# A two-layer mixer trunk in split fp32: order of work between VectorE and ScalarE, two budgets in the planner, smaller weight loads

## The chip, the cores and the metric

One Trainium2 chip, one of its cores. The metric is device time in microseconds of one execution of the program: the median of three executions of the kernel before is 2058.87 us (2057.31 to 2063.75).

## What is computed

Two layers, each on 256 tokens of 2048 channels, all in float32: one RMS norm, one input projection to nine parts, a convolution branch and an attention branch, each gated and projected, and an output projection with the residual.

```python
def conv_branch(a, glu, gate, conv_w, conv_b, ln_g, ln_b):
    u = a * jax.nn.sigmoid(glu)
    u = causal_depthwise_conv(u, conv_w) + conv_b          # 31 taps, 2048 channels
    u = jax.nn.silu(layernorm(u, ln_g, ln_b))
    return u * jax.nn.silu(gate)

def mla_branch(...):
    q = (rmsnorm(q_down, q_a_g) @ w_uq)                    # 16 heads of 192
    kv = (rmsnorm(kv_down, kv_a_g) @ w_ukv)                # 16 heads of 128 + 128
    q, k = rmsnorm(q), rmsnorm(k with shared k_pe)         # per head, then rotary on 64 of 192
    o = chunk_causal_attention(q, k, v)
    return o * jax.nn.silu(gate)

def hybrid_layer(x, ...):
    proj = rmsnorm(x, norm_g) @ w_in
    c_a, c_glu, c_gate, q_down, kv_down, k_pe, m_gate, g_conv, g_mla = split(proj)
    y_conv = conv_branch(...) @ w_proj_conv
    y_mla = mla_branch(...) @ w_proj_mla
    y = sigmoid(g_conv) * y_conv + sigmoid(g_mla) * y_mla
    return x + y @ w_out
```

(The convolution call and the head reshapes are written short here.)

## The kernel before, in words

**Products in split precision.** Each weight matrix is streamed once from HBM. A weight tile is split in two: `hi`, a copy rounded to the matmul's own format (ScalarE, `act.copy`), and `lo`, what the rounding left (VectorE, `vec.tensor_sub` of raw and hi). The activations are split in the same way. A product takes three matmuls for each tile of 128 channels and each half of the 256 tokens: hi by hi, hi by lo, lo by hi.

**Slots.** `product` runs over a block of up to 512 output columns in steps of KS = 2 tiles of the contracted dimension, which is a slot: 2 tiles x 2 token halves x 3 = 12 matmuls. A block of the input projection, of `wpm`, `wpc` and `wo` has 8 slots, one of `wuq` (384 columns) or `wukv` (512) has 2. A layer is the list of blocks in `order_of_layer`: glu 0, three down blocks, glu 1 and 2; then eight times a pair of heads (uq, ukv) with a glu or cgate block between; then cgate 2 and 3, and four blocks each of mgate, gmla, pmla, gconv, pconv and wout. In the slot of step j, `product` first issues the splits of the steps up to j + 2 (`SPLIT_AHEAD`), then the 12 matmuls, then `background`.

**Loads.** `load` brings a piece of KG = 4 tiles, 1 MB at 512 columns, into one of three `raw` buffers, on SP's queue, two pieces ahead. `split_p` has three `hi` and three `lo` buffers, one for each step.

**Everything else rides in the slots.** The class `InOrder` ties the instructions of an engine in the order in which the code traces them, so each engine works through one fixed list. `background(n)` adds a slot to `clock`, runs what is due in `steps` (put there by `at_slot(ahead, f, cost)`), and then, while a budget of VectorE time is positive, takes work from the queue `fill`. The budget of a slot is the time that twelve matmuls are thought to take less that of the low half, and debts are carried over. In `fill` are the 31 taps of the depthwise convolution of each of eight channel blocks (`conv`, `tap`), and behind them the layernorm (`mean`, `centre`, `var`, `factors`, `apply`) and `gated`, which makes the operand `yc` of pconv. A tap is two VectorE instructions (multiply by a channel's weight and add). With `budget["assist"]`, on from the last pair of heads to the next layer's down blocks, ScalarE scales the next tap's input into a tile `tap`, and that tap is one addition on VectorE.

**Transposing.** `turn` parks a tile in DRAM with four DMAs of POOL's queue (`park`), fetches it four slots later (`fetched`) and transposes 32 x 32 blocks on VectorE eight slots after the start (`blockwise`), then calls `use`.

**Attention.** `attention(b)` puts the steps of a pair of heads on slots after its ukv block: statistics (2), scaling (3, which parks qk), fetch (7), transposition (11), rope and nope splits (12, 15), scores (17), maxima (18), exponentials (19), and so on to the outputs (33). A pair begins every 12 slots, so three pairs are under way at a time.

**At pconv** the local function `before` runs `fill` until the channel block that the next step needs has been gated.

Of the kernel before, what the change touches and what calls it, by code (L numbers as in the profile page):

```python
# [12 lines left out]
F32 = mybir.dt.float32  # L13
# [8 lines left out]
T = 2  # L22
# [35 lines left out]
KG = 4  # L58
KS = 2
FIRST_STEPS = ((0, 1), (1, 2), (2, 4))  # L60
N_WARM = 11

# [5 lines left out]
QROT_AT, STATS_AT, SCALE_AT, QK_BACK_AT, QK_TURN_AT, ROPE_AT, NOPE_AT = 1, 2, 3, 7, 11, 12, 15  # L68
SCORES_AT, MAX_AT, EXP_AT, P_BACK_AT, P_TURN_AT, P_SPLIT_AT, VALUES_AT, O_AT = 17, 18, 19, 23, 28, 29, 31, 33
# [47 lines left out]
def trunk(ctx: ExitStack, tc: tile.TileContext, xT, x, g_in, pos, win, wuq, wukv, wpc, wpm, wo, cst, rows, invf, out):  # L117
# [23 lines left out]
    raw_p = pool("raw", 3)  # L141
# [19 lines left out]
    pieces, splits = [], []  # L161

    def plan(layer, stream):
        ap, nk = streams[stream]
        i, at = taken.get((layer, stream), (0, 0))
        n = blocks_of_layer()[stream][i]
        mine = []
        for g in range(nk // KG):
            size = P * KG * n
            pieces.append((ap[layer, at : at + size].rearrange("(p k c) -> p k c", p=P, k=KG), n))  # L170
            at += size
            for h in range(KG // KS):
                splits.append((len(pieces) - 1, h, n))
                mine.append(len(splits) - 1)
        taken[layer, stream] = (i + 1, at)
        return nk, n, mine
# [6 lines left out]
    loaded, done = {}, {}  # L183
    LOAD_AHEAD, SPLIT_AHEAD = 2, 2

    def load(i):
        if i >= len(pieces) or i in loaded:
            return
        ap, n = pieces[i]
        t = raw_p.tile([P, KG, n], F32, tag="raw", name=f"raw{i}")  # L190
        for j, (a, b) in enumerate(FIRST_STEPS if i == 0 else ((0, KG),)):
            if i == 0:
                load_x(j)
            sp.dma_start(t[:, a:b, :], ap[:, a:b, :])
        loaded[i] = t

    def split(i):
        if i >= len(splits) or i in done:
            return
        piece, h, n = splits[i]  # L200
        load(piece)
        r = loaded[piece][:, h * KS : (h + 1) * KS, :]
        hi = split_p.tile([P, KS, n], F32R, tag="hi", name=f"hi{i}")
        lo = split_p.tile([P, KS, n], F32R, tag="lo", name=f"lo{i}")
        step = 1 if i == 0 else KS
        for a in range(0, KS, step):
            if i * KS < NCT:
                for c in range(i * KS + a, i * KS + a + step):
                    first_h(c)
            k = slice(a, a + step)  # L210
            act.copy(hi[:, k], r[:, k])
            vec.tensor_sub(lo[:, k], r[:, k], hi[:, k].bitcast(F32))
        done[i] = hi, lo
        for a in range(1, LOAD_AHEAD + 1):
            load(piece + a)
# [3 lines left out]
    steps, clock = [], [0]  # L219
    fill, budget = deque(), {"us": 0.0, "hold": 0, "assist": False}  # L220

    def at_slot(ahead, f, cost=0.0):
        steps.append((clock[0] + ahead, cost, f))

    def background(n):
        clock[0] += 1
        budget["us"] = min(budget["us"], 0.0) + 12 * (n / 2400 + 0.0133) - (KS * n / 960 + 0.06) - 0.04
        while True:
# [4 lines left out]
            for _, cost, f in due:  # L233
                budget["us"] -= cost
                f()
        while fill and budget["us"] > 0 and clock[0] >= budget["hold"]:
            run_fill()

    def run_fill():
        cost, f, hold = fill.popleft()  # L240
        budget["us"] -= cost
        budget["us"] -= f() or 0.0
        budget["hold"] = clock[0] + hold

    def product(planned, stat, evacuate, evac_at=EVAC_AT, cost=0.0, before=None):
# [7 lines left out]
        for j, i in enumerate(mine):  # L253
            for a in range(SPLIT_AHEAD + 1):
                split(i + a)
# [11 lines left out]
            if j == len(mine) - 1:  # L267
                steps.insert(0, (clock[0] + 1 + evac_at, cost, evac))
# [23 lines left out]
    def turn(src, n, use, dst=None, cost=0.7):  # L292
# [6 lines left out]
        def blockwise():  # L299
            z = back[0]  # L300
            vec.transpose(z if dst is None else dst.rearrange("p c (i s) -> p i c s", i=4), z)
            use(z.rearrange("p i c s -> p c i s"))

        at_slot(TURNED_AT, blockwise, cost)


    def rsqrt(y, ms):
# [7 lines left out]
        for _ in range(3):  # L315
            vec.tensor_mul(t, y, y)
            vec.scalar_tensor_tensor(t, t, -0.5, ms, op0=ALU.mult, op1=ALU.mult)
            vec.scalar_tensor_tensor(y, t, 1.5, y, op0=ALU.add, op1=ALU.mult)

# [92 lines left out]
    for i in range(3, len(x_chunks)):  # L412
        load_x(i)
        if i < len(x_chunks) - 1:
            load(i - 2)
# [18 lines left out]
    for l in range(DEPTH):  # L434
# [25 lines left out]
        def down_after(down=down, qkc=qkc, ss_d=ss_d, r_d=r_d, kpe=kpe, ccq=ccq, ssq_t=ssq_t, gqk=gqk, row=row, C=C):  # L460
# [27 lines left out]
            def separated(c, tps):  # L488
                act.copy(qkc[:, 0, c : c + 2, :], tps[c])
                vec.tensor_sub(qkc[:, 1, c : c + 2, :], tps[c], qkc[:, 0, c : c + 2, :].bitcast(F32))  # L490
# [20 lines left out]
            for t in range(T):  # L511
                at_slot(2 + t, lambda t=t: squares(t))
# [3 lines left out]
            for c, at in ((0, 8), (2, 9), (4, 11), (6, 12)):  # L516
                at_slot(at + 2, lambda c=c: separated(c, tps), 0.7)
# [50 lines left out]

        def ukv_evac(b, t, ps, pair_of=pair_of):
# [5 lines left out]
            vec.tensor_sub(p["vl"][:, t], v, p["vh"][:, t].bitcast(F32))  # L575
            act.copy(p["qk"][:, t, :, 2:4, :], k)
            for h in range(2):
# [6 lines left out]
        def attention(b, pair_of=pair_of, ss_d=ss_d, kpe=kpe, ccq=ccq, ssq_t=ssq_t, gqk=gqk, A=A):  # L584
# [3 lines left out]

            def rotate_q():
                both = lambda a: a.rearrange("p t (a c) -> p (t a) c", a=2).unsqueeze(2).broadcast_to([P, 2 * T, 2, HALF])  # L590
                qa = work.tile([P, T, 2, 2, HALF], F32, tag="qa", name="qa")
                qb = work.tile([P, T, 2, 2, HALF], F32, tag="qb", name="qb")
                qr = p["qr"].rearrange("p t a h c -> p (t a) h c")
                vec.tensor_mul(qa.rearrange("p t a h c -> p (t a) h c"), qr, both(ccq))
                vec.tensor_mul(qb.rearrange("p t a h c -> p (t a) h c"), qr, both(ssq_t))
                out = qk[:, :, :, 4, :].rearrange("p t (h a) c -> p t h a c", h=2)
                vec.tensor_sub(out[:, :, :, 0, :], qa[:, :, 0], qb[:, :, 1])
                vec.tensor_add(out[:, :, :, 1, :], qb[:, :, 0], qa[:, :, 1])
# [38 lines left out]
            def split_nope(which):  # L637
                z = back[:, :, 2 * which : 2 * which + 2, :].rearrange("p b h s -> p h b s")
                hi, lo = (nope_t[:, 2 * which + i].rearrange("p h (b s) -> p h b s", s=32) for i in range(2))
                if which == 0:  # L640
                    act.activation(z, z, AF.Copy, scale=gqk)
                act.copy(hi, z)
                vec.tensor_sub(lo, z, hi.bitcast(F32))

            def split_rope(which):
                z = back[:, :, 4 + which, :]
                rt, rl = (a.rearrange("p i h (b s) -> p i h b s", s=32) for a in (rope_t, rope_l.unsqueeze(1)))
                for h in range(2):
                    own, other = halves[h], halves[1 - h]
                    act.copy(rt[own, which, h], z[own])  # L650
                    if which == 0:
                        vec.tensor_sub(rt[other, 0, h], z[own], rt[own, 0, h].bitcast(F32))
                    else:
                        act.copy(rt[other, 1, h], z[own])
# [521 lines left out]
```

## Time and profile before

| | |
|---|---|
| median of three executions | 2058.87 us |
| the profiled execution, its own time | 2055.45 us |
| its span, first to last instruction | 2053.7 us |
| HBM read and written | 395.51 MB, 40.37 MB |
| ScalarE table loads | 46, 1283 ns each |

The profile is of one execution. PE is TensorE's matmuls, PEld its weight loads, DVE VectorE, ACT ScalarE, POOL GpSimd, SP the engine that issues the loads. A line of a group reads: engine, operation, output <- inputs by the program's tile names, shape, count, busy time, mean of one, and the idle time before it with what ended it. Every instruction passes through the class `InOrder`, so all have the same line number (L128) and are told apart by their tiles: `lo<-raw,hi` is a low half, `hi<-raw` a high half, `v_t<-u_t,cst,v_t` a tap on VectorE, `tap<-u_t,cst` ScalarE's scaling for one.

### The profile page before, as it was taken

The numbers are of one execution on the slowest core, as the hardware profiler recorded it, in microseconds if no ns is written. First come the engines' busy times: TensorE is split into PE (matmuls) and PEld (weight loads), VectorE is DVE, ScalarE is ACT, GpSimd is POOL, SyncE is SP. The second block draws the span as 40 slices with busy tenths as digits, with TensorE's granted clock in tenths as the row PEclk, the third lists the DMA queues.
The fourth block names the chain that finished last, engine by engine and source line by source line (L and its number), as shares of the span: only waits on it lengthen the run. The fifth ranks groups of instructions, "written<-read, shape, count | busy, mean of one in ns | idle before, by whom it ended". The sixth has DMA issues, their size and how long they took to land. (4 is left out here: it accounts for less than half of the span.)

```text
span 2053.7 us, 25692 instructions
## 1 busy us (share of the span) xinstructions
PE 1945.0 (95%) x8787; PEld 1598.1 (78%) x8787; DVE 1615.7 (79%) x2701; ACT 1248.4 (61%) x2136; POOL 370.9 (18%) x694
## 2 busy tenths in 40 slices
PE   9999999999999998999999998998999999989999
PEld 8888778778788876778789887787877887767787
DVE  5888787789999986765669787777888999766654
ACT  6556667777677655534455576677765776454343
POOL 1023333322200000121210232342322000000200
PEclk9999999999999999999999999999999999999999
DMA  8557767766655555566756676776766555545664
GB/s 303 189 195 249 241 202 242 253 221 219 212 205 190 185 185 174 193 225 241 263 190 208 208 250 202 229 241 216 247 206 214 192 185 195 203 153 186 226 219 168
DMA packets 86163, 437.59 MB, mean 213 GB/s; under 512 B 17296, under 2 KB 21136, under 8 KB 47248
## 3 DMA queue, kind: packets, MB, share of 16 engines
q1 hardware_dynamic: 55296, 359.61, 49.7%
q0 software_dynamic: 30304, 76.06, 12.0%
q8 instruction: 69, 1.13, 0.2%
q14 instruction: 62, 0.51, 0.1%
q10 hardware_dynamic: 432, 0.28, 0.0%
HBM read 395.51 MB, written 40.37 MB: 212 GB/s over the span
## 5 line engine op out<-in xcount | busy, mean ns | idle before, releaser
L128 DVE TENSOR_TENSOR lo<-raw,hi 128x1024 fp32r<-128x1024 f32 (+3 forms) x689 | 811.8, 1184 | 336.3 <-ACT hi L128 335.2
L128 ACT CAST hi<-raw 128x1024 fp32r<-128x1024 f32 (+3 forms) x689 | 695.1, 1021 | 486.1 <-PE acc L128 440.0
L128 PE MATMUL acc<-hi,hT 128*128 128x512 f32 (+2 forms) x1728 | 539.6, 389 | 18.2 <-ACT hi L128 18.2
L128 PEld LDWEIGHTS acc<-hi,hT 128*128 128x128 f32 x1728 | 326.8, 190 | 87.2 <-ACT hi L128 27.6
L128 PE MATMUL acc<-lo,hT 128*128 128x512 f32 (+2 forms) x864 | 338.7, 392 | 27.4 <-DVE lo L128 27.2
L128 PE MATMUL acc<-lo,h_hi 128*128 128x512 f32 (+2 forms) x864 | 338.1, 391 | 26.6 <-DVE lo L128 26.5
L128 PE MATMUL acc<-hi,h_hi 128*128 128x512 f32 (+2 forms) x864 | 336.0, 389 | 14.7 <-ACT hi L128 14.7
L128 PE MATMUL acc<-hi,h_lo 128*128 128x512 f32 (+2 forms) x864 | 333.2, 386 | 0.0
L128 DVE SCALAR_TENSOR_TENSOR v_t<-u_t,cst,v_t 128x256 f32<-128x256 f32 x608 | 263.4, 481 | 4.2 <-ACT v_t L128 0.8
L128 PEld LDWEIGHTS acc<-lo,h_hi 128*128 128x128 f32 x864 | 163.7, 189 | 72.1 <-DVE lo L128 42.5
L128 PEld LDWEIGHTS acc<-lo,hT 128*128 128x128 f32 x864 | 164.4, 190 | 71.2 <-DVE lo L128 41.8
L128 PEld LDWEIGHTS acc<-hi,h_hi 128*128 128x128 f32 x864 | 163.7, 189 | 52.6 <-ACT hi L128 22.5
L128 PEld LDWEIGHTS acc<-hi,h_lo 128*128 128x128 f32 x864 | 163.6, 189 | 29.2
L128 PE MATMUL acc<-hi,ycT 128*128 128x512 f32 x512 | 159.5, 390 | 4.9 <-ACT hi L128 4.9
L128 PE MATMUL acc<-hi,yT 128*128 128x512 f32 x512 | 159.6, 390 | 2.0 <-ACT hi L128 2.0
L128 PE MATMUL acc<-hi,oT 128*128 128x512 f32 x512 | 158.3, 390 | 0.0
L128 ACT ACTIVATE tap<-u_t,cst 128x256 f32<-128x256 f32 x352 | 158.2, 501 | 0.0
L128 POOL DMA_DIRECT2D turned<-turn_d x82 | 46.0, 560 | 604.4 <-ACT sq L128 411.0
L128 POOL DMA_DIRECT2D turn_d<-gate x176 | 95.9, 552 | 324.6 <-DVE gate L128 270.7
L128 PE MATMUL acc<-hi,qkc 128*128 128x512 f32 (+1 forms) x512 | 147.3, 363 | 0.0
L128 DVE TENSOR_TENSOR v_t<-v_t,tap 128x512 f32<-128x512 f32 x176 | 121.3, 689 | 12.8 <-ACT tap L128 5.1
L128 PEld LDWEIGHTS acc<-hi,ycT 128*128 128x128 f32 x512 | 96.1, 188 | 27.1 <-ACT hi L128 7.4
(165 smaller groups left out, 2254.1 us busy)
## 6 DMA issues: line engine op xcount, KB each, us to landing
raw<-in_win SPq DMA_DIRECT2D x191, 1024.0 KB, 5.2
raw<-in_wpm SPq DMA_DIRECT2D x32, 1024.0 KB, 4.8
raw<-in_wpc SPq DMA_DIRECT2D x32, 1024.0 KB, 4.8
raw<-in_wo SPq DMA_DIRECT2D x32, 1024.0 KB, 4.9
raw<-in_wukv SPq DMA_DIRECT2D x16, 1024.0 KB, 5.6
turned<-turn_d POOLq DMA_DIRECT2D x50, 256.0 KB, 3.9
raw<-in_win SPq DMA_DIRECT2D x16, 768.0 KB, 4.4
raw<-in_wuq SPq DMA_DIRECT2D x16, 768.0 KB, 4.2
```

What stands on the lines that cost most here:

```text
L128: ins = getattr(self.engine, name)(*a, **k)
```

## The change

Five things, in one diff.

1. *Loads and splits.* A piece is now KS = 2 tiles, half as large; `raw` has five buffers. `split` becomes `split_hi` and `split_lo`: the high half is issued three slots ahead, with a fourth `hi` buffer, the low half two.

```diff
-KG = 4
 KS = 2
-    raw_p = pool("raw", 3)
+    raw_p = pool("raw", 5)
-    LOAD_AHEAD, SPLIT_AHEAD = 2, 2
+    LOAD_AHEAD, HI_AHEAD, LO_AHEAD = 4, 3, 2
+        highs[i] = split_p.tile([P, KS, pieces[i][1]], F32R, tag="hi", name=f"hi{i}", bufs=4)
...
-            for a in range(SPLIT_AHEAD + 1):
-                split(i + a)
+            for a in range(HI_AHEAD + 1):
+                split_hi(i + a)
+                if a <= LO_AHEAD:
+                    split_lo(i + a)
```

2. *Two budgets, and order in the slot.* Costs are pairs (VectorE, ScalarE). `late` holds what is traced last in the slot. `soon` puts a step in the next slot and lets it be called earlier (`pay`). Items of `fill` carry a condition: a mark and a number of slots after it.

```diff
-    fill, budget = deque(), {"us": 0.0, "hold": 0, "assist": False}
+    fill, budget, marks, owed = deque(), {"vec": 0.0, "act": 0.0}, {}, []
+    def soon(f, vec=0.0, act=0.0):
+        owed.append(f)
+        at_slot(1, lambda: pay(f), vec, act)
+    def pay(upto):
+        while upto in owed:
+            owed.pop(0)()
     def background(n):
         clock[0] += 1
-        budget["us"] = min(budget["us"], 0.0) + 12 * (n / 2400 + 0.0133) - (KS * n / 960 + 0.06) - 0.04
+        slot = 12 * (n / 2400 + 0.0133) - 0.04
+        for e, split_us in (("vec", KS * n / 960 + 0.06), ("act", KS * n / 1066 + 0.04)):
+            budget[e] = min(budget[e], 0.0) + slot - split_us
...
-        while fill and budget["us"] > 0 and clock[0] >= budget["hold"]:
+        while fill and budget["vec"] > 0 and budget["act"] > 0:
+            after, slots = fill[0][1]
+            if after and clock[0] < marks.get(after, 1 << 30) + slots:
+                break
             run_fill()
+        finish_late()
     def run_fill():
-        cost, f, hold = fill.popleft()
...
+        f, (after, _) = fill.popleft()
+        while owed and after and after not in marks:
+            owed.pop(0)()
+        spend(f() or (0.0, 0.0))
```

3. *VectorE's part of a pair of steps is moved.* To the end of the slot (`late`): the rest of v in `ukv_evac`, of p in `split_p`, of qkc in `separated`, the glu product with its parks, the mgate product with its parks, the rests in `four` and of oT. To the next slot: the rests of rope and nope (`split_rope`, `split_nope`), what follows a transposition (`turn` with `then`), the squares after `centre` (ScalarE), the SiLU after `apply` (ScalarE), the split of yc after `gated`. For example:

```diff
             def split_p():
                 act.copy(hi, z)
-                vec.tensor_sub(lo, z, hi.bitcast(F32))
+                late.append(lambda: vec.tensor_sub(lo, z, hi.bitcast(F32)))
...
             def apply(b):
                 v = vs[b][:, :, :SEQ]
                 vec.tensor_mul(v, v, wide(rstd))
-                for j in range(2):
-                    act.activation(... AF.Silu ...)
+                def silu():
+                    for j in range(2):
+                        act.activation(... AF.Silu ...)
+                    mark(("silu", b))
+                soon(silu, 0.0, 1.1)
+                return 0.6, 0.0
```

The steps of attention move with it: rope from 12 to 14, the fetch of p from 23 to 24, its transposition from 28 to 29, values from 31 to 32, outputs from 33 to 34; `rotate_q` now follows uq by two slots instead of ukv by one.

4. *Taps.* ScalarE scales the next tap wherever its budget is above 0.8, in any stage; the first tap goes from ScalarE to VectorE.

```diff
                 if k == 0:
                     for j in range(2):
-                        act.activation(v[:, j, :SEQ], u[:, j, :SEQ], AF.Identity, bias=bias, scale=weight(k, j))
+                        vec.tensor_scalar(v[:, j, :SEQ], u[:, j, :SEQ], weight(k, j), bias, op0=ALU.mult, op1=ALU.add)
...
-                    if budget["assist"] and k + 1 < CONV_W:
-                        scale(k + 1)
+                if budget["act"] > 0.8 and 0 < k < CONV_W - 1:
+                    scale(k + 1)
+                    costs = (costs[0], 0.85)
```

5. *The order of the tail.* The gates of the first two channel blocks are fetched and transposed before the layernorm ends; the reciprocal root is cut into four items; only four `apply` stand ahead of the first `gated`; `before_pconv` takes the place of `before`.

```diff
+        def before_pconv(j, keep=keep):
+            c = j * KS // 4
+            while c not in keep["separated"]:
+                run_fill()
+            pay(keep["separated"][c])
+            finish_late()
```

Costs of the steps, as (VectorE, ScalarE): glu (0.9, 2.2), uq (0, 2.3), ukv (0.75, 2.6), rope (0, 2.5) and 1.65 in the next slot, nope (0, 1.8) and 1.2, exponentials (0, 3.3), cgate (0, 2.0), mgate (1.25, 1.4), gmla (0, 2.7), gconv (0, 3.9), pmla (1.25, 0), pconv (2.4, 0), wout (1.25, 1.5).

More of the change, by code (lines that the diff above doesn't have):

```diff
@@ new lines, in trunk, with at_slot, spend, mark @@
+    steps, clock, late = [], [0], []
+    fill, budget, marks, owed = deque(), {"vec": 0.0, "act": 0.0}, {}, []
+    def at_slot(ahead, f, vec=0.0, act=0.0):
+        steps.append((clock[0] + ahead, (vec, act), f))
+    def spend(costs):
+        budget["vec"] -= costs[0]
+        budget["act"] -= costs[1]
+    def soon(f, vec=0.0, act=0.0):
[4 more added lines that the diff above has]
+            owed.pop(0)()
+    def mark(name):
+        marks[name] = clock[0]
@@ L267, in product @@
             if j == len(mine) - 1:
-                steps.insert(0, (clock[0] + 1 + evac_at, cost, evac))
+                steps.insert(0, (clock[0] + 1 + evac_at, costs, evac))
             background(n)
@@ L875, in layernorm @@
+            then(var, after=("squared", 7), slots=1)
+            then(factors, after="var", slots=1)
+            for _ in range(3):
+                then(more_factors)
+            for b in range(4):
+                then(apply, b)
             for c in range(4):
                 if c < 2:
-                    fill.append((0.0, lambda c=c: ahead(c + 2), 0))
+                    then(ahead, c + 2)
                 for t in range(T):
-                    fill.append((1.4 + 1.2 * t, lambda c=c, t=t: gated(c, t, gates[c][t]), 0))
@@ L880, in layernorm, with turn4 @@
-                fill.append((0.0, lambda c=c: keep.update(gated=c), 0))
-        def turn4(src, c, use, cost):
+                    if c > 1:
+                        then(turned_gate, c, t)
+                    then(lambda c, t: gated(c, t, gates[c][t]), c, t, after=("silu", 2 * c + 1), slots=1)
+                for b in (4 + 2 * c, 5 + 2 * c) if c < 2 else ():
+                    then(apply, b)
+        def turn4(src, c, use, *costs):
             if c < 3:
-                return turn(src, 512, use, cost=0.65 + cost)
+                return turn(src, 512, None, then=use, then_costs=costs)
```

350 lines of the change are left out of this document (189 added, 161 removed).

## The prediction

> **What bounds the kernel now.** I read first the page's busy times, then who TensorE and VectorE waited for, then TensorE by stage, and last the instructions inside one stalled stretch.
>
> ```profile
> PE 1945.0 (95%) x8787; PEld 1598.1 (78%) x8787; DVE 1615.7 (79%) x2701; ACT 1248.4 (61%) x2136; POOL 370.9 (18%) x694
> ```
> ```profile
> PE acc L128 <- DVE lo L128: 62.2, 91, 1.0
> PE acc L128 <- ACT hi L128: 39.8, 43, 2.8
> ```
> ```profile
> DVE lo L128 <- ACT hi L128: 335.2, 259, 4.5
> ...
> DVE qk L128 <- DMA qk<-turn_d: 2.4, 1, 2.4
> ```
>
> TensorE sets the time, but it waits 102 us, in 134 short pieces, for the two halves of the split weights, never for a load. VectorE and ScalarE are not full. VectorE stands 335 us in front of a low half because ScalarE has not written the high half: both belong to the same slot, so whatever holds ScalarE holds VectorE. Where this costs time is seen by stage (columns: window, its length, each engine's busy time and instructions, granted clock, DMA share, GB/s):
>
> ```profile
> core 0: us, PE busy (x) PEld busy (x) DVE busy (x) ACT busy (x) POOL busy (x), PEclk, DMA share, GB/s
> 129.70:403.40 273.70, 257.19 (x1213) 214.90 (x1213) 224.16 (x464) 190.80 (x416) 96.77 (x181) 0.99 0.68 231
> 403.40:644.60 241.20, 230.93 (x1030) 188.11 (x1030) 218.29 (x336) 171.25 (x283) 41.97 (x77) 0.99 0.63 213
> 733.20:933.10 199.90, 184.41 (x777) 145.46 (x776) 136.47 (x174) 97.89 (x120) 20.82 (x38) 0.99 0.58 200
> 1146.30:1424.60 278.30, 260.79 (x1214) 217.22 (x1213) 223.57 (x461) 191.57 (x418) 96.03 (x179) 0.98 0.68 227
> 1424.60:1667.60 243.00, 232.46 (x1029) 189.49 (x1028) 217.75 (x337) 169.55 (x279) 42.69 (x79) 0.99 0.62 212
> 1756.90:1959.50 202.60, 184.24 (x778) 144.29 (x777) 128.35 (x156) 94.64 (x112) 20.80 (x38) 1.00 0.56 198
> 1060.00:1076.00 16.00, 16.00 (x94) 16.00 (x93) 7.66 (x10) 8.46 (x12) 1.84 (x4) 1.00 0.61 212
> ```
> The windows are attention; cgate 2 to gmla; gconv and pconv, in each layer; the last row is a clean run of 384-wide matmuls, 0.17 us each. The chain of waits gives the clean 512-wide pace and the length of a head pair:
>
> ```profile
> 1207.18 1.89 PE s L128 x16
> ...
> 1479.21 1.89 PE s L128 x16
> ...
> 1970.16 79.00 PE acc L128 x347
> ```
> 79.00/347 is 0.228 us a matmul, so a slot of twelve is **2.73 us**. From the first to the eighth set of scores seven pairs pass in 272 us, 38.9 each. Clean, a pair is 24 x 0.17 + 120 x 0.228 + 1.9 of scores + at most as much for the values = 35.3. So **attention loses at least 3.6 us a pair, 57 in 16 pairs**. The stage after it has 80 slots, 218.6 us, with about 7 us of the last pairs' matmuls: it loses 15.6 and 17.4, **33** in all. gconv and pconv are 64 slots, 174.9 us: they lose 25.0 and 27.7, **53**.
>
> How a slot stalls is plain in gconv, here VectorE and then ScalarE:
>
> ```profile
> 810.78 0.69 DVE L128 TENSOR_TENSOR v_t<-v_t,ln_stats 128x512 f32<-128x512 f32 x1
> 813.56 1.22 DVE L128 TENSOR_TENSOR lo<-raw,hi 128x1024 fp32r<-128x1024 f32 x1 [2.10 <-ACT hi L128]
> ```
> ```profile
> 811.50 1.09 ACT L128 ACTIVATE v_t<-v_t,cst 128x256 f32<-128x256 f32 x2 [1.90 <-DVE v_t L128]
> 812.50 1.03 ACT L128 CAST hi<-raw 128x1024 fp32r<-128x1024 f32 x1
> 813.55 1.28 ACT L128 ACT_TABLE_LOAD   x1
> ```
> VectorE multiplies, ScalarE waits for that and applies SiLU, then makes the next high half, and only then VectorE can make the low half: four steps in series, 3.9 us instead of 2.73, while each engine alone has under 2.2 us of work.
>
> **The change part by part.** *Order.* The low half is issued for two slots ahead and the high half for three, so it no longer meets its own slot's ScalarE work; what VectorE takes from ScalarE in a slot is traced last in it (`late`) or a slot later (`soon`, the inner `at_slot(1, ...)`). No arithmetic goes away.
>
> In attention the heaviest run on VectorE are the three slots 2 to 4 after ukv: statistics 2.2, scaling 1.1, rope rests 1.65, nope rests 1.2 by the costs in the code, with three low halves of 1.22 (row below) 9.8 us against three slots of 2.73. VectorE falls 1.6 behind, and being two slots ahead forgives 2 x 2.73 - 1.22 = 4.2. What can still stop TensorE is the scores, which now follow the nope rests by one slot instead of two, and the qk round trip through DRAM, which keeps its four slots between fetch and transposition while these get shorter; so far it made VectorE wait once, 2.4 us. I keep 1.0 us a pair and book 2.6 x 16 = **42**. Bounds: 57 if nothing is left, 16 if only 1 us a pair is won.
>
> From cgate 2 to gmla the gates' products and the oT rest are taken apart in the same way. VectorE is busy there 218.29 and 217.75 us, nine tenths, so I book somewhat over half of the 33: **19**; bounds 30 and 5.
>
> *Both engines counted.* Now a conv tap is traced only where both budgets are positive, and ScalarE scales the next tap wherever it has 0.8 us left, no longer only after the last pair.
>
> ```profile
> L128 DVE SCALAR_TENSOR_TENSOR v_t<-u_t,cst,v_t x608: 443/480/497, 85.1 to 1754.4; 128x256 f32<-128x256 f32 x152
> L128 DVE TENSOR_TENSOR v_t<-v_t,tap x176: 654/689/696, 433.9 to 1755.0; 128x512 f32<-128x512 f32 x176
> L128 ACT ACTIVATE v_t<-u_t,cst x32: 587/597/623, 81.9 to 1710.7; 128x256 f32<-128x256 f32 x32
> L128 DVE TENSOR_TENSOR v_t<-v_t,ln_stats x32: 684/685/693, 759.1 to 1829.2; 128x512 f32<-128x512 f32 x32
> L128 ACT ACTIVATE v_t<-v_t,cst x32: 583/589/604, 798.7 to 1830.4; 128x256 f32<-128x256 f32 x32
> L128 DVE TENSOR_TENSOR v_t<-turned,v_t x32: 419/424/429, 826.3 to 1861.3; 128x256 f32<-128x256 f32 x32
> L128 ACT CAST ycT<-v_t x16: 614/620/624, 829.3 to 1862.0; 128x512 fp32r<-128x512 f32 x16
> L128 DVE TENSOR_TENSOR ycT<-v_t,ycT x16: 684/689/693, 829.9 to 1862.7; 128x512 fp32r<-128x512 f32 x16
> ```
> ```profile
> L128 DVE TENSOR_TENSOR lo<-raw,hi 128x1024 fp32r<-128x1024 f32 x607 | 736.3, 1219 | 265.4 <-ACT hi L128 264.5
> L128 ACT CAST hi<-raw 128x1024 fp32r<-128x1024 f32 x607 | 629.2, 1049 | 404.2 <-PE acc L128 381.4 <-issue 6.7 <-ACT hi L128 5.4
> ...
> L128 ACT ACTIVATE tap<-u_t,cst 128x256 f32<-128x256 f32 x352 | 158.2, 501 | 0.0
> ```
> I went through both planners slot by slot with the costs and budgets of the code and no durations. For the kernel before, 91 and 85 taps of the two layers come out with ScalarE's help: 176, as the second row has it, and the last tap of layer 0 in gconv's fifth slot. For the kernel after I get 159 + 158 = **317** helped taps and 163 without help (326 instructions instead of 608); the 32 first taps go to VectorE. A tap without help is 2 x 0.48, one with help 0.69, so VectorE saves about 23 us if a first tap costs it no more than 0.48, and ScalarE takes 141 x 0.90 (158.2 us over 176 taps) = 127 more and gives up 32 x 0.60: **+108 us**. ScalarE has 805 us free, so most of this is hidden. If every slot took two scalings it would be 1.05 + 1.80 = 2.85 against 2.73, 0.12 over; in the 159 slots that 317 scalings then fill that is 19 us. The budget drops what is left of a slot, so I book **-4**, bounds 0 and -19.
>
> *The price of the second condition.* A slot in which ScalarE is in debt takes no tap, though VectorE has room: attention takes 30 and 31 taps instead of 40 and 41. The last tap falls in gconv's 16th slot in layer 0 (before: 5th) and in the 11th in layer 1 (before: the last slot but two of pmla). From mean to the first gated product it then takes 13 slots in layer 0 and 17 in layer 1; when pconv begins, 18 and 11 items are still in `fill`, and `before_pconv` traces them without a budget, ahead of the block that needs them. This burst is not covered: it stands on VectorE behind a low half that goes into the buffer of the block just finished, so it starts when TensorE is already free. At the third block of layer 0: low half 1.22, two scalings by rstd 2 x 0.69, from the first of them two blocks of SiLU on ScalarE 2 x 1.09, two casts 0.62 each, the last rest 0.69: about 1.9 + 2.2 + 1.2 + 0.7 = 6.0 us. By the same rows the first, fifth and seventh blocks cost about 4.5, 6 and 5, and in layer 1 the third, fifth and seventh 3, 5 and 5. Together **34 us**. So of the 53 lost in gconv and pconv now, the ping-pong goes but the burst comes: I leave 50 and book **3**; bounds 34 + 3 = 37 if the burst hides, and -25 if it costs nearly twice as much.
>
> The clock of the windows is 0.98 to 0.99 in attention and 1.00 in the clean run. The Trainium skill, TensorE: Matmul & The Clock Gate, Part 1, states that an idle window of about 3.4 us halves TensorE's clock until a busy one. By that rule seven waits of 3 to 6 us would each bring up to 1.7 us more, 12 in all, and the sum would be 2011.
>
> *Loads of two K tiles.* Each megabyte becomes two halves; three buffers of four tiles become five of two, so SP issues twice as many loads, each behind its own low half.
>
> ```profile
> raw<-in_win SPq DMA_DIRECT2D x191, 1024.0 KB, 5.2
> ...
> raw<-in_win SPq DMA_DIRECT2D x8, 640.0 KB, 3.9
> ```
> From these two rows half a megabyte should land within 3.9 us (an estimate). It is issued when VectorE has done the low half two slots ahead and is cast four slots later: 10.9 us, less 1.2 and VectorE's lag. Hidden: 0, and if that cover were gone a load could cost up to its 3.9 us. The Trainium skill, DMA: Bandwidth & Descriptors, section Bandwidth, speaks against it: batch to 1 MiB or more for three quarters of the peak. By its fit of 2.0 us plus bytes over 436 GB/s half a megabyte takes 3.2 us, which is hidden too, so the sum stays.
>
> *The rest*: the fourth high buffer only lets ScalarE be three slots ahead; rotate_q a slot earlier, the rsqrt in steps, the gates transposed before the layernorm's end: the same instructions elsewhere, booked at 0. On POOL the parks of su and gate come at the end of their slot, behind which stand the fetches for four slots later.
>
> **Sum**: 42 + 19 + 3 - 4 = 60. The profiled execution took 2055.45 us (span 2053.7), 3.4 less than the median of 2058.87. From the one 1995, from the other 1999: I predict **2000**.
>
> **Rivals.** (1) *The burst hides*, because VectorE and ScalarE are further ahead at pconv than I count: 34 more, 1966. For it: both are under 70% busy in gconv and pconv now. Against it: three low buffers bind VectorE to TensorE. (2) *Attention keeps its stalls under another name*: the qk fetch stands on POOL behind the parks of the exponentials, VectorE waits 2 us a pair: 32 less, 2032. Only one such wait now, but the slots get a tenth shorter. (3) *ScalarE becomes the bound* in the tap slots: 19 lost, of which 4 are booked, and half of attention's 42: 2000 + 15 + 21 = 2036; with all of attention's gain gone 2057, no difference that counts. (4) *Slower*: the conv slips further than the slot count says. From a last tap later than gconv's 24th slot on, centring, variance and rstd fall into the burst too; some 14 slots of 2.73, 38 us, are laid bare per layer, 76 in all: 2000 + 76 = 2076. My count leaves 8 slots to that point in layer 0.
>
> **How the numbers follow.** Forecast 0.47 (1980 to 2022), (1) 0.22 (1950 to 1980), (2) 0.15 (2022 to 2042), (3) 0.08, (4) 0.08. 1955 to 2048 leaves out (4) and a few hundredths at each end. A difference under 0.3%, 6 us, cannot be told from none here: faster 0.87; same 0.05, the upper end of (3); slower 0.08.
>
> **What would show it.** Right: VectorE's wait for ScalarE at lo falls from 335 us to under 100; a pair takes 36 to 37 us; 317 tap additions; in pconv's first block waits of TensorE of 3 to 6 us at every second slot. Wrong: waits of ScalarE for raw (loads late), TensorE stalled on hi in gmla and pmla (ScalarE full), pair times near 39, or TensorE running through pconv's first block.

## The result, and the profile after

The kernel after takes **1962.42 us**, the median of four runs (1960.77 to 1963.85); the kernel before took 2059.82 us in the same comparison (four runs, 2057.31 to 2063.75). The ratio is 0.9525, 95% interval 0.9508 to 0.9543. Forecast were 2000 us and a range of 1955 to 2048: direction and range held, the size was 38 us short. The profiled run took 1963.85 us, span 1961.9.

First the busy times on the page, then who TensorE waited for, then two of VectorE's waits (total us, times, longest):

```profile
PE 1912.8 (97%) x8787; PEld 1607.8 (82%) x8787; DVE 1598.0 (81%) x2592; ACT 1350.8 (69%) x2385; POOL 371.1 (19%) x694
```
```profile
PE acc L127 <- ACT ycT L127: 31.7, 7, 5.6
PE s L127 <- DVE qk_t L127: 6.8, 18, 1.9
PE acc L127 <- DVE lo L127: 2.8, 7, 0.7
...
PE acc L127 <- ACT hi L127: 0.7, 1, 0.7
```
```profile
DVE lo L127 <- ACT hi L127: 29.1, 24, 2.2
...
DVE qk L127 <- DMA qk<-turn_d: 11.2, 12, 2.8
```

TensorE's 102 us of waits for split weights have shrunk to 3.5; seven long waits for `ycT`, the operand of pconv, have come instead. VectorE's wait for the high half fell from 335.2 to 29.1 us. The stages, in the columns shown before:

```profile
127.20:380.40 253.20, 250.50 (x1213) 214.10 (x1212) 216.57 (x435) 197.30 (x435) 97.22 (x181) 1.00 0.77 252
380.40:606.80 226.40, 226.05 (x1029) 188.16 (x1029) 208.33 (x308) 180.65 (x303) 41.57 (x76) 1.00 0.68 226
693.90:900.30 206.40, 186.23 (x777) 151.81 (x776) 147.90 (x197) 111.01 (x151) 20.82 (x38) 0.93 0.57 189
1103.80:1361.30 257.50, 252.64 (x1213) 215.31 (x1212) 216.93 (x433) 199.79 (x440) 97.07 (x181) 0.99 0.76 247
1361.30:1587.70 226.40, 226.06 (x1030) 188.19 (x1030) 208.63 (x309) 181.00 (x305) 41.67 (x77) 1.00 0.69 226
1674.70:1869.80 195.10, 183.54 (x778) 150.13 (x777) 139.97 (x181) 105.17 (x138) 20.82 (x38) 0.96 0.61 202
```

Attention and the stage after it are far shorter; gconv and pconv (third and sixth row) are as long as before, with TensorE idle 20 and 12 us and a granted clock of 0.93 and 0.96. The next table cuts every trace at the same matmuls of the program and adds the two layers (us; each column is one profiled run):

| stage | before | after | splits alone | free taps | order undone |
|---|---|---|---|---|---|
| heads (glu, down) | 249.1 | 242.6 | 243.5 | 242.0 | 247.2 |
| attention | 551.7 | 510.6 | 518.5 | 511.6 | 558.6 |
| cgate 2 to gmla | 484.4 | 453.0 | 467.3 | 454.9 | 479.5 |
| pmla | 177.8 | 174.1 | 177.8 | 181.5 | 174.1 |
| gconv and pconv | 402.6 | 401.4 | 361.9 | 351.9 | 422.0 |
| wout | 188.0 | 180.1 | 180.6 | 180.1 | 187.8 |
| span | 2053.7 | 1961.9 | 1949.5 | 1922.0 | 2069.2 |

The last three columns are experiments told below.

**The burst at pconv.** TensorE's first matmuls of a slot after each wait, from the timeline (start, length, what, and in brackets the idle time before it and who ended it):

```profile
788.09 0.79 PE L127 MATMUL acc<-hi,ycT 128*128 128x512 f32 x1 [5.24 <-ACT ycT L127]
...
800.61 0.80 PE L127 MATMUL acc<-hi,ycT 128*128 128x512 f32 x1 [5.03 <-ACT ycT L127]
...
814.15 0.79 PE L127 MATMUL acc<-hi,ycT 128*128 128x512 f32 x1 [5.55 <-ACT ycT L127]
...
826.58 0.80 PE L127 MATMUL acc<-hi,ycT 128*128 128x512 f32 x1 [4.35 <-ACT ycT L127]
```
```profile
1771.32 0.71 PE L127 MATMUL acc<-hi,ycT 128*128 128x512 f32 x1 [2.13 <-ACT ycT L127]
...
1783.75 0.79 PE L127 MATMUL acc<-hi,ycT 128*128 128x512 f32 x1 [5.08 <-ACT ycT L127]
...
1796.07 0.79 PE L127 MATMUL acc<-hi,ycT 128*128 128x512 f32 x1 [4.35 <-ACT ycT L127]
```

Forecast were waits of 4.5, 6, 6, 5 and 3, 5, 5, 34 in all; they are 5.24, 5.03, 5.55, 4.35 and 2.13, 5.08, 4.35, together 31.7. The chain behind the second one, on VectorE and on ScalarE:

```profile
795.45 1.23 DVE L127 TENSOR_TENSOR lo<-raw,hi 128x1024 fp32r<-128x1024 f32 x1 [1.58 <-PE acc L127]
796.59 1.28 DVE L127 TENSOR_TENSOR v_t<-v_t,ln_stats 128x512 f32<-128x512 f32 x2
...
800.59 1.29 DVE L127 TENSOR_TENSOR ycT<-v_t,ycT 128x512 fp32r<-128x512 f32 x2 [1.37 <-ACT ycT L127]
```
```profile
796.68 1.28 ACT L127 ACT_TABLE_LOAD   x1
797.97 2.08 ACT L127 ACTIVATE v_t<-v_t,cst 128x256 f32<-128x256 f32 x4
799.96 1.12 ACT L127 CAST ycT<-v_t 128x512 fp32r<-128x512 f32 x2
```

The low half starts when TensorE has ended its slot, then come the scalings by rstd, a table load, SiLU and the casts. It is the series that the forecast had, with two differences. ScalarE's table load is not in the forecast: the first scaling is done at 797.27, SiLU starts at 797.97, after the load. And TensorE starts at 800.61, when the first cast has ended at 800.56; it does not wait for the second cast (to 801.08) and for the last rest, which the forecast had counted.

The waits are not the whole price. The windows in which the clock then stood at a half:

```profile
785.00:791.80 6.80, 3.71 (x9) 2.89 (x10) 3.27 (x6) 6.11 (x10) 1.09 (x2) 0.50 0.47 155
...
1795.30:1802.20 6.90, 6.13 (x15) 4.75 (x16) 2.67 (x5) 1.75 (x3) 0.00 (x0) 0.51 0.03 10
sum 44.60, PE 34.14 PEld 26.47 DVE 15.98 ACT 16.31 POOL 1.09; mean PE 4.88 PEld 3.78 DVE 2.28 ACT 2.33 POOL 0.16
```

In the seven stretches that follow the seven waits TensorE works 34.14 us at half speed and loses half of that, 17.1 us. **The burst costs 31.7 + 17.1 = 48.8 us.**

### The profile page after: what moved, and what is told of

Same layout as the page of the kernel before. It is cut to its first block, busy times and chain, and to the rows that moved or that the text cites. A ratio compares the mean times of both kernels' runs of the same rounds, so it can differ in the third digit from the quotient of the medians.

```text
span 1961.9 us, 27462 instructions
## 1 busy us (share of the span) xinstructions
PE 1912.8 (97%) x8787; PEld 1607.8 (82%) x8787; DVE 1598.0 (81%) x2592; ACT 1350.8 (69%) x2385; POOL 371.1 (19%) x694
## 5 line engine op out<-in xcount | busy, mean ns | idle before, releaser
L127 ACT CAST hi<-raw 128x1024 fp32r<-128x1024 f32 (+3 forms) x689 | 703.4, 1024 | 525.1 <-PE acc L127 441.3
L127 PE MATMUL acc<-hi,hT 128*128 128x512 f32 (+2 forms) x1728 | 525.9, 383 | 0.0
L127 PE MATMUL acc<-lo,h_hi 128*128 128x512 f32 (+2 forms) x864 | 331.1, 383 | 2.8 <-DVE lo L127 2.8
L127 PE MATMUL acc<-hi,h_hi 128*128 128x512 f32 (+2 forms) x864 | 331.3, 383 | 0.7 <-ACT hi L127 0.7
L127 PE MATMUL acc<-lo,hT 128*128 128x512 f32 (+2 forms) x864 | 330.7, 383 | 0.1
L127 ACT ACTIVATE tap<-u_t,cst 128x256 f32<-128x256 f32 x634 | 274.9, 499 | 0.0
L127 DVE TENSOR_TENSOR v_t<-v_t,tap 128x512 f32<-128x512 f32 x317 | 218.4, 689 | 21.2 <-ACT tap L127 4.7
L127 PE MATMUL acc<-hi,ycT 128*128 128x512 f32 x512 | 171.1, 415 | 31.7 <-ACT ycT L127 31.7
L127 PEld LDWEIGHTS acc<-hi,ycT 128*128 128x128 f32 x512 | 103.5, 202 | 58.0 <-ACT ycT L127 34.7
L127 DVE SCALAR_TENSOR_TENSOR v_t<-u_t,cst,v_t 128x256 f32<-128x256 f32 x326 | 140.9, 479 | 1.4
```

Source lines behind the costliest of these rows:

```text
L127: ins = getattr(self.engine, name)(*a, **k)
```

## The experiments

In each comparison the kernel before ran beside the others; its medians there are 2055.44 to 2057.58 us, against 2059.82 above, so differences of 2 or 3 us between runs of different comparisons decide nothing. Every variant of the kernel after also clears the marks at the start of each layer. That alone, as a kernel of its own:

```diff
     for l in range(DEPTH):
+        marks.clear()
```

> The kernel after with the marks cleared at the start of each layer and nothing else, the base of all variants of it. In the kernel after, layer 1 still finds the marks of layer 0 and so waits no slot between the layernorm's links. Theory (the tail of layer 1 is set by the last tap, not by these slots): 1959-1967, gconv and pconv of layer 1 within 3 us of 195.2. Rival (the slots count): that stage 5 us longer or more, 1968 or more, and the variants' losses would be too large by so much.

1965.86 us (1960.42 to 1967.4; ratio 0.9545, 0.9531 to 0.956); gconv and pconv of layer 1 take 194.9 us. The theory holds, and the variants can be compared with the kernel after.

**Free taps.** Is it the second condition that makes the conv late?

```diff
-        while fill and budget["vec"] > 0 and budget["act"] > 0:
+        while fill and budget["vec"] > 0 and (budget["act"] > 0 or fill[0][1][1] < 0):
...
-                fill.append((lambda k=k: tap(k), (None, 0)))
+                fill.append((lambda k=k: tap(k), (None, -1)))
```

> The kernel after, with one condition changed: a conv tap is taken from the fill queue whenever VectorE's budget is positive, also when ScalarE is in debt. Theory (the burst at pconv comes from the second condition): counted slot by slot, the last tap now falls in gconv's first block in layer 0 and in pmla in layer 1, nothing is left in the queue when pconv begins, TensorE's 31.7 us of waits for ycT and the half-speed clock behind them go: 1915 to 1930 us. Rival (those taps fill the slots that kept VectorE ahead, and attention stalls again): the ycT waits go, but waits for lo or qk_t of 20 us or more come back: 1945 to 1965.

1925.68 us (1924.01 to 1926.34), ratio 0.9357 (0.9343 to 0.9371): **36.7 us less than the kernel after**. The windows of gconv and pconv of both layers:

```profile
699.40:875.20 175.80, 175.80 (x777) 145.40 (x776) 128.89 (x163) 98.08 (x114) 19.73 (x36) 1.00 0.68 222
1654.00:1830.10 176.10, 176.10 (x779) 145.82 (x777) 122.83 (x152) 95.75 (x113) 19.72 (x36) 1.00 0.68 223
```

No idle time, clock 1.00, and 175.8 and 176.1 us for 64 slots, forecast at 174.9 clean. The stage falls by 49.5 us, which is the 48.8 of waits and clock. TensorE's busy time in it falls by 17.9 us (186.23 and 183.54 to 175.80 and 176.10), which bears out the 17.1 for the clock. Part of the gain is paid back in pmla, 174.1 to 181.5 in the table: in layer 0 VectorE is busy 88.2 of 91.5 us there, and TensorE's weight loads wait 5.2 us for low halves. VectorE does more taps alone (428 multiply-and-add instructions for 326, 266 additions of a scaled input for 317); outside pmla no other stage grows by more than 1.9 us.

**Three parts of the order, each undone in the kernel after.** What is late is traced at once:

```diff
-    steps, clock, late = [], [0], []
+    class Now(list):
+        def append(self, f):
+            f()
+    steps, clock, late = [], [0], Now()
```

> The kernel after, but what is put in late is issued at once, in the place where the kernel before had it; budgets, slots and look-ahead stay. Theory (the order inside the slot is worth much): VectorE stands in front of ScalarE in its own slot again, 20 to 40 us are lost in attention and in the stage after it: 1980 to 2000. Rival (the high half being one slot further ahead already does all of it): within 5 us of the kernel after.

1977.93 us (1975.66 to 1979.02; ratio 0.9611, 0.9595 to 0.9628): 15.5 more, between the two expectations. By stage it is all attention, 525.1 for 510.6; no other moves by 2 us. It is not the wait that the theory named: VectorE's wait for the high half is 24.5 us (29.1 in the kernel after), while TensorE's wait for `qk_t` at the scores rises from 6.8 to 17.7.

The high half two slots ahead as the low half, three buffers:

```diff
-    LOAD_AHEAD, HI_AHEAD, LO_AHEAD = 4, 3, 2
+    LOAD_AHEAD, HI_AHEAD, LO_AHEAD = 4, 2, 2
-        highs[i] = split_p.tile([P, KS, pieces[i][1]], F32R, tag="hi", name=f"hi{i}", bufs=4)
+        highs[i] = split_p.tile([P, KS, pieces[i][1]], F32R, tag="hi", name=f"hi{i}")
```

> The kernel after with the high half two slots ahead instead of three and three hi buffers instead of four. Theory (the extra slot takes lo off its own slot's ScalarE work): VectorE's wait for hi at lo rises from 29 to over 150 us and the time by 20 to 40 us: 1980 to 2000. Rival (the moved steps alone keep ScalarE free at the slot's start): within 6 us.

1987.71 us (1986.2 to 1989.18; ratio 0.9659, 0.9645 to 0.9674): 25.3 more, the theory's case; attention is 10.1 longer, the heads and gconv with pconv about 5 each, cgate 2 to gmla 2.0. VectorE's wait at lo is back to almost all of the 335 us of before, and yet TensorE hardly waits for the two halves:

```profile
DVE lo L127 <- ACT hi L127: 311.1, 216, 5.1
```
```profile
PE acc L127 <- DVE lo L127: 4.1, 8, 0.8
PE acc L127 <- ACT hi L127: 1.7, 2, 1.3
```

So this wait of VectorE, on which the forecast's first sign rested, does not by itself show lost time.

The moved steps back in the slot of the step ahead of them:

```diff
     def soon(f, vec=0.0, act=0.0):
-        owed.append(f)
-        at_slot(1, lambda: pay(f), vec, act)
+        spend((vec, act))
+        f()
...
-                at_slot(1, lambda: then(z), *then_costs)
+                spend(then_costs)
+                then(z)
```

(the rests of `split_rope` and `split_nope` alike)

> The kernel after with every moved step back in the slot of the step ahead of it: soon and the inner at_slot(1) are called at once; late, loads, budgets stay. Late and the second high half showed nothing between cgate 2 and gmla, where 31 us went. Theory (the moved steps are what won there): that stage takes 10-15 us more in each layer, attention 2-5 more, 1985-2005 in all. Rival (ScalarE's own budget won there, by keeping taps out of full slots): that stage stays within 3 us, 1962-1972 in all.

1940.45 us (1938.49 to 1945.94; ratio 0.9425, 0.9405 to 0.9445): **22 us less**, outside both expectations. Neither attention (511.1) nor cgate 2 to gmla (453.8) notices; the gain is all in gconv and pconv:

```profile
694.10:895.60 201.50, 184.74 (x776) 150.30 (x775) 144.75 (x190) 109.59 (x149) 20.82 (x38) 0.95 0.60 194
1672.90:1852.00 179.10, 177.28 (x778) 145.63 (x777) 137.94 (x178) 103.57 (x133) 20.83 (x38) 1.00 0.67 220
```

Layer 1 loses its burst almost wholly, layer 0 keeps most of it. So moving steps a slot later cost time just where the conv was late, and won nothing elsewhere as long as the rest of the order stood. Two things change at once here, and they were not taken apart: each link of the layernorm's chain comes a slot earlier, and so does the last tap, which starts 38.9 and 22.0 us after gconv instead of 43.4 and 28.6.

**Does moving steps cost by itself?** The same edit on the kernel with free taps:

> Free taps and the moved steps back in their own slot. With the taps under both budgets that move cost 22 us, all of it in gconv and pconv. Theory (it costs only there where the conv's end is late, since each link of the layernorm's chain then stands a slot further from pconv): gconv and pconv 175-177 us in each layer as in the run with free taps, 1920-1929 in all, no difference. Rival (a step a slot later costs or gains VectorE time by itself): 1915 or less, or 1935 or more.

1929.25 us (1926.58 to 1931.07; ratio 0.9375, 0.9359 to 0.9391), a hair above the theory's range; that kernel itself came to 0.9357 and 0.9376. No difference in all: gconv and pconv take about 177.5 in each layer. Single stages do shift, attention about 4 us shorter, the heads, cgate 2 to gmla and gconv with pconv about 3 longer each, but once the conv is in time the move neither costs nor wins in the sum.

**All three undone together**, with the budgets, the taps and the tail of the kernel after:

> The kernel after with late, soon, the inner at_slot(1) and the third high half ahead all undone together; the two budgets, the taps and the tail stay. Theory (each part covers for the others, since one wait has several causes): more than the three losses by themselves (15.5 and 25.3 and that of the run with moved steps back) together, by at least 10 us, 2025-2055. Rival (the parts add up): the sum of the three losses within 6 us, 2005-2025.

2070.54 us (2067.43 to 2071.27; ratio 1.0058, 1.0039 to 1.0076), 0.6% **above the kernel before**: the whole gain is gone. The three losses add up to 15.5 + 25.3 - 22.0 = 18.8, and together they cost 108. VectorE's wait, TensorE's waits for the halves and the attention window are much as before again:

```profile
DVE lo L127 <- ACT hi L127: 341.7, 252, 5.2
```
```profile
PE acc L127 <- DVE lo L127: 69.3, 65, 2.7
...
PE acc L127 <- ACT hi L127: 18.0, 22, 1.8
```
```profile
128.00:405.20 277.20, 257.22 (x1213) 216.07 (x1212) 216.77 (x435) 197.78 (x434) 97.20 (x181) 0.98 0.70 228
```

The theory's direction, and far more than it expected: any two parts cover for most of the third. In the run with the high half two ahead VectorE's wait of 311 us went with 5.8 us of TensorE's waits for the halves; here one of 342 us goes with 87.3. That a single part is enough is shown below for the distance of the high half alone; `late` and `soon` alone were not run.

**The splits alone**: the kernel before with part 1 only (pieces of two tiles, five raw and four hi buffers, `split_hi` three ahead, `split_lo` two), planner and taps untouched. The core of the edit:

```diff
-            for a in range(SPLIT_AHEAD + 1):
-                split(i + a)
+            for a in range(HI_AHEAD + 1):
+                split_hi(i + a)
+                if a <= LO_AHEAD:
+                    split_lo(i + a)
```

> The kernel before with part 1 alone: pieces of two tiles, five raw and four hi buffers, the high half three slots ahead, the low half two; planner, taps and all other order as before. Theory (the two halves no longer meet in one slot): VectorE's wait at lo for hi falls from 335 us to under 120 and the time to 2018-2038, the gain in attention and from cgate 2 to gmla. Rival (the pairs of steps in series inside a slot hold both engines all the same): the wait at lo moves to other steps and the time is 2046-2060.

1951.42 us (1950.48 to 1954.4; ratio 0.9484, 0.9467 to 0.9502): 106 us less than before and **11 less than the whole change**. Both expectations missed; the theory's mechanism is there, three times as large. VectorE's wait, then attention, cgate 2 to gmla, and gconv with pconv of layer 0:

```profile
DVE lo L128 <- ACT hi L128: 33.4, 25, 4.2
```
```profile
126.90:384.50 257.60, 251.55 (x1213) 212.72 (x1212) 224.52 (x462) 189.99 (x417) 97.16 (x181) 1.00 0.76 247
384.50:619.80 235.30, 229.13 (x1029) 188.59 (x1028) 216.03 (x334) 170.96 (x283) 41.58 (x76) 0.99 0.68 215
708.60:889.10 180.50, 177.52 (x777) 145.02 (x776) 135.18 (x174) 98.14 (x120) 20.82 (x38) 1.00 0.68 219
```

One slot of distance between the halves takes away most of the wait in every stage, and in gconv the ping-pong, the steps in series between VectorE and ScalarE that the forecast found there; 36.6 us of TensorE's waits for low halves are left. Part 1 also halves the loads, but they don't bring this: the run with all three parts undone has the same small loads and is no faster than the kernel before. Over the splits alone the kernel after leads by 14.3 us from cgate 2 to gmla, 7.9 in attention and 3.7 in pmla, and loses 39.5 in gconv and pconv.

**Larger loads**, the run with the high half two ahead given pieces of four tiles and three raw buffers:

```diff
-KS = 2
+KG, KS = 4, 2
-    raw_p = pool("raw", 5)
+    raw_p = pool("raw", 3)
```

> e3 (high half two ahead, three hi buffers) with the loads of the kernel before: pieces of four tiles, 1 MB, in three raw buffers. Theory (half loads are hidden either way and only make room for the fourth hi buffer): within 6 us of e3. Rival (smaller loads come earlier and gain by themselves): 10 us or more slower than e3; rival of the skill (large loads move faster): 10 us or more faster.

1993.32 us (1990.03 to 1998.64; ratio 0.9689, 0.9668 to 0.971), 5.6 more than with half a megabyte: just within the theory's 6 us, and neither rival's case. Large loads are no faster here.

**Where help pays.** Free taps, but ScalarE scales only where it did before:

```diff
-                if budget["act"] > 0.8 and 0 < k < CONV_W - 1:
+                if helps["on"] and 0 < k < CONV_W - 1:
...
                 attention(i)
+                helps["on"] = i == NPAIR - 1
```

> The run with free taps, but ScalarE scales taps only where it did in the kernel before (from the last pair of heads to the next layer's down blocks). By the planner's bookkeeping about 340 helped taps, the last one in gconv's fourth slot in layer 0, 4 items left at pconv. Theory (help in attention is worth little, VectorE has a fifth of its time free): 1922-1938, attention within 4 us of the run with free taps. Rival (help in attention is what keeps VectorE in time): attention 8-15 us longer in each layer, 1945 or more.

1937.97 us (1937.22 to 1939.53; ratio 0.9418, 0.9401 to 0.9434). The upper end of the theory: attention is 1.0 us longer, but cgate 2 to gmla takes 465.6 for 454.9:

```profile
382.40:615.70 233.30, 228.96 (x1029) 187.41 (x1028) 215.60 (x303) 210.90 (x394) 41.59 (x76) 1.00 0.68 217
1343.90:1576.10 232.20, 229.45 (x1030) 187.70 (x1029) 215.47 (x303) 213.25 (x398) 42.04 (x77) 1.00 0.67 219
```

Most of the help falls on that stage, and ScalarE is as full there as VectorE, nine tenths each. Spread over the layer it is worth 10.7 us there, or somewhat less: this run also has 120 taps a layer in that stage, the one with free taps 110.

**More help**: free taps, and ScalarE scales whenever it is not in debt; beside it the run with free taps once more.

```diff
-                if budget["act"] > 0.8 and 0 < k < CONV_W - 1:
+                if budget["act"] > 0 and 0 < k < CONV_W - 1:
```

> The run with free taps once more, beside the next one: 1924-1928.

> Free taps, and ScalarE scales the next tap wherever it is not in debt (above 0 instead of above 0.8). In pmla the run with free taps has VectorE busy 88.2 of 91.5 us. Theory (VectorE bounds pmla there): more helped taps (about 320 by the planner's bookkeeping for 266), the last tap some four slots earlier, pmla 2-4 us shorter in each layer, 1917-1923. Rival (scalings make ScalarE late for the high halves): 1926 or more, TensorE waiting at hi.

1926.51 us (1924.31 to 1930.33; ratio 0.9376, 0.9362 to 0.9389) for free taps, 1931.22 us (1929.51 to 1931.85; ratio 0.9394, 0.9381 to 0.9408) with more help. The help came as counted (321 helped taps, the last one four slots earlier in layer 0), the gain did not. It is the rival's time, at the edge of what can be told from no difference, and by another wait than it named: TensorE waits only 3.7 us at hi, but VectorE now stands for the scaled inputs, 14.3 us (below) for 3.7, and pmla is 183.6, no shorter than 181.5.

```profile
DVE v_t L127 <- ACT tap L127: 14.3, 17, 2.0
```

The fastest kernel of the study is the one with free taps, 0.9357 and 0.9376 in two comparisons.

## Why the forecast held, and where it was short

The forecast booked 60 us; the spans differ by 91.8. The missing 31.8 are, by its own terms:

- **Attention, 42 booked, 41.1 measured.** The first sets of scores of pairs 1 and 8 of layer 1 start at 1158.50 and 1411.66: 253.2/7 = 36.2 us a pair, where 36 to 37 were named.

```profile
1158.50 0.72 PE L127 MATMUL s<-qk_t 128*128 128x256 f32 x2
...
1411.66 2.05 PE L127 MATMUL s<-qk_t 128*128 128x256 f32 x16
```

  The residue of 1 us a pair was well judged. The forecast put the gain on distance and moved work together; shown is that part 1 alone, the distance, brings 33.2 of it in the kernel before, and that without distance, the high half two ahead, the moved work still brings 37.9 of the 48.0 us between all undone (558.6) and all done (510.6).
- **cgate 2 to gmla, 19 booked for the order, 31.4 measured.** The distance gives 17.1 (484.4 to 467.3), the whole order with free taps and ScalarE's help where it was before gives 18.8 (to 465.6): the order brought what was booked. Most of the rest belongs to the taps: help moved out of this stage brings up to 10.7. The reason given for booking only part of the 33 was wrong all the same. With free taps VectorE is even fuller than nine tenths, 214.52 of 227.10 us, and TensorE stands for 0.7 us:

```profile
380.80:607.90 227.10, 226.42 (x1030) 188.09 (x1029) 214.52 (x328) 181.78 (x307) 41.58 (x76) 1.00 0.69 223
```

- **Taps, -4 booked.** This step failed by its sign. The count was exact:

```profile
L127 DVE SCALAR_TENSOR_TENSOR v_t<-u_t,cst,v_t x326: 445/479/488, 82.1 to 1698.7; 128x256 f32<-128x256 f32 x163
L127 DVE TENSOR_TENSOR v_t<-v_t,tap x317: 650/692/697, 84.0 to 1703.3; 128x512 f32<-128x512 f32 x159
L127 DVE TENSOR_SCALAR v_t<-u_t,cst x32: 404/408/414, 80.3 to 1662.1; 128x256 f32<-128x256 f32 x32
```

  317 helped taps, 326 instructions for the rest, 32 first taps at 0.41 us. The price was not: the +102 us on ScalarE are hidden, and they relieve VectorE in the stage above, 208 us of work for 218. In pmla too, for which the forecast had no term, the kernel is 3.7 us shorter: it takes about as many taps as before, 60 a layer for 61, but 45 of them with help for 31. With free taps, where 18 to 20 a layer go without help for 15, pmla takes 181.5.
- **gconv and pconv, 3 booked, 1.2 measured**, both halves measured apart. The ping-pong is worth 50.7 (402.6 to 351.9, free taps), where 53 were found lost. The burst was put at 34 us of waits and measured 31.7; what it costs beyond that is the clock. That 3 and 1.2 lie so close is partly luck: of the 50 us left to this stage, 34 were the burst's waits and 16 a reserve without a row behind it, and the clock's 17.1, which the forecast had put beside its sum and not into it, filled that reserve.
- **Heads and wout, nothing booked, 14.4 measured** (6.5 and 7.9). The second step that failed is the list of stages: wout took 94.0 us a layer for 32 slots of 2.73, 87.4, and the forecast never held it against the clean pace. The splits alone bring 13.0 of it.
- **Loads, 0 booked**: hidden. Half a megabyte of `win` lands in 4.3 us, estimated at no more than 3.9 from the rows. The fit that the forecast took from the Trainium skill, DMA: Bandwidth & Descriptors, is stated there for DMAs issued by GpSimd, not SP, and gave 3.2; the measured time decides. ScalarE waits for a load ten times, 10.3 us in all (4.3 before), TensorE never.

```profile
raw<-in_win SPq DMA_DIRECT2D x383, 512.0 KB, 4.3
```

cgate 2 to gmla is 12.4 above what was booked, pmla's 3.7 stand in place of the -4 (7.7), and the heads and wout bring 14.4: 34.5 together. Attention and the conv stages give 2.7 back.

**The clock.** The rule of the Trainium skill, TensorE: Matmul & The Clock Gate, Part 1, gave 2011 for the sum, with 12 us more for the burst. In the burst the trace agrees and goes further, 17.1 us. Neither sum had a term for the other side: the trace of the kernel before has ten stretches of 3.4 us at half clock, each worth up to 1.7, and the kernel after has one outside the burst, the kernel with free taps none in one profiled run and one in the other. Up to 15 us of the gains listed above are these (9 x 1.7).

**The rivals.** The time is that of rival 1, the burst that hides, 1966, but its mechanism is refuted: the burst came in full. Rival 2 (qk's round trip) fell: VectorE waits 11.2 us for it in all, TensorE 6.8 for qk_t. Rival 3 (ScalarE the bound) fell: TensorE waits 0.7 us for a high half. Rival 4 needed a last tap eight slots later than counted; but the run with free taps shows that the conv's deadline was the weak place.

## What to carry to other kernels

Where two in-order engines hand work to each other once per slot, give the producer one slot of distance first: here that one edit brought 106 of the some 130 us by which the fastest kernel of the study beats the kernel before. The other cures of the same stalls stood in for it more than they added to it. A budget condition on queued work is a delay; before adding one, count when the last item must be done and what the chain behind it still needs. Hold every stage against its clean pace before pricing a change, the short ones too, and price a stall in the clock as well as in its own length.

## What the runs showed of the hardware

The clock falls without an idle window. In the kernel before, this window of 3.4 us is followed by one at half clock, though TensorE's two gaps in it are below 1 us each:

```profile
1197.50:1200.90 3.40, 1.66 (x7) 0.91 (x6) 2.42 (x8) 3.37 (x7) 0.00 (x0) 1.00 0.00 0
1200.90:1204.30 3.40, 3.40 (x10) 2.62 (x9) 3.10 (x11) 1.53 (x3) 0.00 (x0) 0.50 0.63 231
```
```profile
1198.80 0.50 PE L128 MATMUL acc<-hi,hT 128*128 128x512 f32 x1 [0.98 <-ACT hi L128]
...
1200.06 0.50 PE L128 MATMUL acc<-lo,hT 128*128 128x512 f32 x1 [0.76 <-DVE lo L128]
```

The clock's record in each trace changes on a grid of 3.41 us. Over all fourteen traces of this case, a full-speed window with TensorE busy below 1.48 us was always followed by half clock, one above 1.84 us never; a half-speed window led back to full speed only with 2.84 us or more busy; at 2.79 and less it was followed by another. In the kernel after, the six waits of 4.35 to 5.55 us were each followed by 6.8 us at half clock, the one of 2.13 us by 3.4. The place on the grid counts as well: in the run with the marks cleared two waits of 4.35 us brought 3.4 each. The Trainium skill, TensorE: Matmul & The Clock Gate, Part 1, names an idle window as the cause; in these traces one less than about half busy is enough.
